# Weight tiles of 256-column products: the first of a block on the activations' remainder of 256 bytes, the later ones 64 bytes off

## The chip, the cores and the metric

The kernel runs on one core of one Trainium2 chip. The metric is the device time of one launch in microseconds. Before the change it is 2145.89 us, the median of three runs from 2144.37 to 2147.65. The profile is of one further execution of the same program, which took 2144.94 us.

## What is computed

The reference is a trunk of two layers in fp32 on 512 tokens of width 2048: first a multi-scale retention with 8 heads, then a latent attention (MLA) with 16 heads. Each layer is normalised, modulated by a conditioning vector, multiplied by a SiLU gate and added to its input. What bears on the change are the two input projections:

```python
def retention_branch(h, pos, w_in, gn_g, w_out):
    proj = h @ w_in                                   # 2048 -> q, k, v, g
    q, k, v, g = jnp.split(proj, [RET_QK, 2 * RET_QK, 2 * RET_QK + RET_WIDTH], axis=-1)
...
def mla_branch(h, pos, w_in, q_norm_g, w_uq, kv_norm_g, w_ukv, w_out):
    proj = h @ w_in                                   # 2048 -> cq, ckv, k_rope, g
    cq, ckv, k_rope, g = jnp.split(
        proj, [MLA_Q_RANK, MLA_Q_RANK + MLA_KV_RANK, MLA_Q_RANK + MLA_KV_RANK + MLA_ROPE], axis=-1)
...
    return (jax.nn.silu(g) * o) @ w_out
```

## The kernel before

Every fp32 product is made of three products in a shorter format: each operand is split into a high part (a cast on ScalarE, ACT) and a low part (the difference, on VectorE, DVE), and high x high, high x low and low x high are added in PSUM. On TensorE each is a weight load (PEld in the profile) of 128x128 and a matmul (PE) that moves 512 or 256 columns of the activations.

Most projections save one product in eight by a scheme of seven block products. For queries and keys of the retention heads 2 to 5 (names qk2 to qk5) and for the gate columns of MLA groups 2 and 3 (g22 and g23) the scheme halves the tokens too, so its matmuls move 256 columns. `seven_rows_steps` makes these six blocks; for every other projection the matmuls move 512 columns, apart from some ends of sums.

A block of `seven_rows_steps` has eight steps, four of a first half (`second` false, u = 0 to 3) and four of a second half. A step of the first half has two weight tiles, e and o, of 1024 columns each in a high and a low copy; it issues four groups of 12 matmuls, named after their PSUM banks: x and s with tile e, z and y with tile o (x, y, s, z in the last of the four). A step of the second half has three groups: x and s with tile o, y with the half-wide tile e (x, s, y in the last). So a block has 4 x 48 + 4 x 36 = 336 matmuls. A name as qk_02e in the profile is head block, first half, u = 2, tile e; the profile leaves the head's number out, so that qk_02e stands for four tiles, and g_02e for two. The 12 matmuls of a group are two row blocks i, two column blocks b and the three partial products (line 924).

Tiles are prepared a step or so ahead: SP issues the loads, ACT casts the high part, DVE forms differences and the low part. The first product with a tile waits for ACT's part; the third one, which is the first that reads the low part, waits for DVE's. The order of ACT, DVE, TensorE and SP is written out by hand (`queued`, `behind`), with these steps one behind the other.

A high and a low copy lie in one pair tile of 2 x 1024 + 16 floats. `part_tiles` takes from a ring of three pair tiles in the base pool and every fourth time from one of the layer's own pool, and `parts_of` begins both copies `at` floats into their half:

```python
EVEN, ASIDE = 16, 0

def pair_tile(pool, tag, name):
    return pool.tile([P, 2 * 1024 + EVEN], F32R, tag=tag, bufs=1, name=name)

def parts_of(pair, shape, at):
    n = math.prod(shape[1:])
    views = [pair[:, 1024 * i + at : 1024 * i + at + n] for i in range(2)]
```

In the built program all activation tiles of these blocks (hT, h2 and their sums) begin 192 bytes past a multiple of 256, and every pair tile 128 bytes past one. A weight tile at EVEN (16 floats, 64 bytes) therefore has the activations' remainder of 256 bytes, and one at ASIDE lies 64 bytes below it. Column blocks are 512 bytes wide and row blocks 1024 or 2048, so the remainder is the same within a tile. Products of 512 columns have their weights at EVEN. The 256-column products of `seven_rows_steps` all have them at ASIDE.

Other places with 256 columns: `tail_block` (line 1406, end of the retention's output) goes through three weight tiles on the activations' remainder and one ASIDE, three matmuls each; `ga_half` (line 1675, the first MLA gate group) follows it with all weights ASIDE.

Between the groups stands little else for TensorE: the head blocks are followed by the 512-column products of the same head (lines 825 to 827, names vg), g22 follows the latent projection (same lines, names vgc) and g23 follows g22. In g23 16 transposes of the latent queries stand behind step u = 2 of the first half and 16 of the latent keys and values behind step u = 0 of the second (line 1790). In g22 the latent norms (lines 1771 to 1774 and 129) run on ACT and DVE between the weight tiles.

Of the kernel before, what the change touches and what calls it, by code (L numbers as in the profile page):

```python
# [16 lines left out]
P = 128  # L17
T = 512
# [31 lines left out]
def hybrid_trunk_kernel(  # L50
# [53 lines left out]
    def tmp(name, shape=(P, T)):  # L104
        return base.tile(list(shape), F32, tag="tmp", bufs=6, name=name)

    def acc(name):
        return psum.tile([P, T], F32, tag="acc", bufs=4, name=name)
# [41 lines left out]
    def rows(w, u, n, c0, cn):  # L150
        return w[u * n * P : (u + 1) * n * P, c0 : c0 + cn].rearrange("(k p) n -> p k n", p=P)
# [67 lines left out]
    EVEN, ASIDE = 16, 0  # L219
# [581 lines left out]
    def turns(raw_tags, own):  # L801

        n = [0, 0]

        def raw_tile(shape, name):
            n[0] += 1
            pool, tag, bufs = raw_tags[n[0] % len(raw_tags)]
            return pool().tile(shape, F32, tag=tag, bufs=bufs, name=f"{name}_r")

        def part_tiles(shape, name, at):  # L810
            n[1] += 1
            return parts_of(next_pair(name) if n[1] % 4 else own(name), shape, at)

        return raw_tile, part_tiles
# [88 lines left out]

        return [step(second, u) for second in (False, True) for u in range(KD // 2)]

    def seven_rows_steps(name, load_half, acts, sums, raw_tile, part_tiles, finish, rows):


        x_, s_, y_, z_, m1, m4, m5 = ([] for _ in range(7))

        def moving(n, p):
            if isinstance(n, tuple):
                kt, th = n
                return tuple(acts[2 * p + kt][:, a, th * H : (th + 1) * H] for a in range(2))
            s = sums[2 * p + (n - 1) // 2]
            return tuple(s[:, (n - 1) % 2, a, :] for a in range(2))

        def product(bank, n, u, w, first):
            for i in range(2):
                a = moving(n, 2 * u + i)  # L920
                for b in range(2):
                    o = bank[:, b * H : (b + 1) * H]
                    for k, (wp, ap) in enumerate(((0, 0), (0, 1), (1, 0))):
                        PE.matmul(  # L924
                            o, w[wp][:, i, b * P : (b + 1) * P], a[ap], start=first and i + b + k == 0, stop=k == 2,
                            skip_group_check=True,
                        )

        def put_by(ps, n):
            m = tmp(n)  # L930
            ACT.copy(m, ps)
            return m

        def parted_halves(hl, n):
            return [tuple(a[:, :, j * H : (j + 1) * H] for a in hl) for j in range(n)]

        def step(second, u):
            n = f"{name}_{int(second)}{u}"
            w = {}

            def load():
                w["o"] = w["e"] = None
                for key, odd_ in (("o", 1), ("e", 0)) if second else (("e", 0), ("o", 1)):
                    js = (1,) if second and key == "e" else (0, 1)
                    w[key] = raw_tile([P, 2, T] if len(js) == 2 else [P, T], f"{n}{key}")
                    v = w[key] if len(js) == 2 else w[key].rearrange("p (i n) -> p i n", i=2)
                    for c, j in enumerate(js):
                        nc.sync.dma_start(v[:, :, c * H : (c + 1) * H], load_half(u, odd_, j))

            def prepare():  # L950
                e, o = w["e"], w["o"]
                if not second:
                    e0, e1, o0, o1 = (t[:, :, j * H : (j + 1) * H] for t in (e, o) for j in range(2))
                    eh, el = part_tiles([P, 2, T], f"{n}e", ASIDE)
                    DVE.tensor_sub(e1, e1, e0)
                    ACT.copy(eh, e)
                    DVE.tensor_sub(o1, o1, e1)
                    DVE.tensor_sub(o0, o0, o1)
                    DVE.tensor_sub(el, e, eh.bitcast(F32))
                    oh, ol = part_tiles([P, 2, T], f"{n}o", ASIDE)  # L960
                    ACT.copy(oh, o)
                    DVE.tensor_sub(ol, o, oh.bitcast(F32))
                    w["b11"], w["t1"] = parted_halves((eh, el), 2)
                    w["t4"], w["t2"] = parted_halves((oh, ol), 2)
                else:
                    oh, ol = part_tiles([P, 2, T], f"{n}o", ASIDE)
                    ACT.copy(oh, o)
                    ev = e.rearrange("p (i n) -> p i n", i=2)
                    DVE.tensor_sub(ev, o[:, :, H:], ev)
                    DVE.tensor_sub(ol, o, oh.bitcast(F32))  # L970
                    eh, el = part_tiles([P, T], f"{n}e", ASIDE)
                    ACT.copy(eh, e)
                    DVE.tensor_sub(el, e, eh.bitcast(F32))
                    w["b21"], w["b22"] = parted_halves((oh, ol), 2)
                    w["t3"] = tuple(a.rearrange("p (i n) -> p i n", i=2) for a in (eh, el))

            def multiply():
                if not second:
                    if u == 0:
                        for l, t in ((x_, "x"), (s_, "s"), (z_, "z"), (y_, "y")):  # L980
                            l.append(acc(f"{t}_{name}"))
                    forms = [(x_, (0, 0), "b11"), (s_, 1, "t1"), (z_, (1, 1), "t4"), (y_, 2, "t2")]
                    if u == NU7 - 1:
                        forms = [forms[i] for i in (0, 3, 1, 2)]
                else:
                    forms = [(x_, (1, 0), "b21"), (y_, 3, "t3"), (s_, 4, "b22")]
                    if u == NU7 - 1:
                        forms = [forms[i] for i in (0, 2, 1)]
                for l, f, k in forms:
                    product(l[0], f, u, w[k], not second and u == 0)  # L990

            def follow():
                if not second and u == NU7 - 1:
                    m1.append(put_by(x_[0], f"m1_{name}"))
                    DVE.tensor_add(y_[0], y_[0], m1[0])
                    m5.append(put_by(s_[0], f"m5_{name}"))
                    DVE.tensor_add(s_[0], y_[0], m5[0])
                if second and u == 0:
                    m4.append(put_by(z_[0], f"m4_{name}"))
                if second and u == NU7 - 1:  # L1000
                    finish(x_[0], s_[0], y_[0], m4[0], m5[0])

            return Step(load, prepare, multiply, follow, rows=rows(second, u))

        NU7 = KD // 4
        return [step(second, u) for second in (False, True) for u in range(NU7)]

    def heads_steps(h):
# [22 lines left out]
    sums2 = {}  # L1031
# [46 lines left out]
    for h in range(1, RH):  # L1078
        if h == 1:
# [4 lines left out]
                sums=lambda u: {0: 2, 1: 3, 2: 4, 4: 5, 5: 6, 6: 7}.get(u),  # L1084
# [428 lines left out]
    h2 = [None] * KD  # L1513
# [128 lines left out]
    def l2_pair(name):  # L1642
        return l2_ready.pop() if l2_ready else pair_tile(pools["l2"], "own", name)
# [161 lines left out]
    turns2 = turns(((lambda: pools["l2"], "bw", 2), (lambda: base, "raw", 3)), lambda name: l2_pair(name))  # L1805
# [5 lines left out]
    def g2_seven(gi):  # L1811


        def load_half(u, odd_, j):
            c0 = 1088 + gi * T + j * H
            return w_mla_in[:, c0 : c0 + H].rearrange("(u i e p) n -> u e p i n", i=2, e=2, p=P)[u, odd_]

        def finish(x, s, y, m4, m5):
            def store(j, half, t):
                r0 = (gi * 4 + 2 * j) * P  # L1820
                POOL.dma_start(
                    sg2_d[r0 : r0 + 2 * P, half * H : (half + 1) * H].rearrange("(b p) n -> p b n", p=P),
                    t.rearrange("p (b n) -> p b n", b=2),
                )

            for j, ps in enumerate((x, s)):
                st = tmp(f"sgs_{gi}_{j}")
                ACT.activation(st, ps, AF.Silu)
                store(j, 0, st)
            for j, m in enumerate((m4, m5)):  # L1830
                DVE.tensor_add(m, m, y)
                ACT.activation(m, m, AF.Silu)
                store(j, 1, m)

        return seven_rows_steps(f"g2{gi}", load_half, h2, sums2, *turns2, finish, lambda second, u: 0)

    g23 = g2_seven(2) + g2_seven(3)

    for n, g_c, at in (("q", qn_s, (0, 4, 10, 11)), ("kv", kvn_c, (1, 5, 12, 13))):
# [655 lines left out]
```

## Time and profile before

| | |
|---|---|
| median of three runs | 2145.89 us |
| lowest and highest | 2144.37, 2147.65 us |
| profiled execution, its own time | 2144.94 us |
| span from first to last instruction | 2143.2 us |
| granted TensorE clock over the span | 0.999 |
| TensorE matmuls and weight loads | 11100 each |
| HBM read and written | 417.96 MB, 43.00 MB |
| matmuls of line 924 | 2016 |

Times in the profile are counted from the span's start. A row of the timeline has the start, the time from the first start to the last end, engine, line, operation, output and inputs, shape and count, and in brackets the engine's idle time before it and what ended it. Matmuls overlap, one's duration is several times the distance to the next, so the speed of a run is read from the starts of two rows and the count between them. In the view by stretch a row has, for each engine, the busy time and the instructions, then the granted clock, the share of the DMA engines and the GB/s that they moved.

### The profile page before, as it was taken

The page shows a single profiled execution, that of the slowest core. Times are in us where ns is not written, and L with a number is a line of the kernel's source. Part 1 is how long each engine was busy: PE and PEld are TensorE (multiplying, and loading weights), DVE is VectorE, ACT ScalarE, POOL GpSimd, SP SyncE. Part 2 cuts the span into 40 slices and gives each one's busy share as a digit, 9 for nine tenths or more (in the row PEclk, how much of TensorE's full clock was granted, in tenths as well). Part 3 has the DMA queues.
Part 4 walks back from the last instruction along what each step waited for, and adds up shares of the span by engine and source line. Part 5 has one row for each costly group of instructions (what it writes and reads, how often), then busy time and mean ns, then how long its engine had stood idle before and what let it go on. Part 6 is the DMA issues. An engine that isn't in the chain of part 4 may idle for free.

```text
span 2143.2 us, 29960 instructions
## 1 busy us (share of the span) xinstructions
PE 2115.7 (99%) x11100; PEld 1816.8 (85%) x11100; DVE 1677.3 (78%) x2481; ACT 1054.5 (49%) x1604; POOL 106.6 (5%) x178
## 2 busy tenths in 40 slices
PE   7999999999999999999999999999999999999998
PEld 5887898988889888888888888898889989988887
DVE  7899788888988789666777777668978788886755
ACT  5764444444444544434344534445446565664434
POOL 1000000000000000000000000010001000000000
PEclk9999999999999999999999999999999999999999
DMA  9975787877788778855647566553466644346734
GB/s 381 397 281 196 223 287 228 273 242 262 252 261 261 236 239 278 262 180 189 236 155 251 178 206 243 167 177 113 163 191 203 188 128 148 119 133 220 246 103 144
DMA packets 229781, 462.95 MB, mean 216 GB/s; under 512 B 20817, under 2 KB 84337, under 8 KB 225793
## 3 DMA queue, kind: packets, MB, share of 16 engines
q1 hardware_dynamic: 217424, 421.85, 60.0%
q0 software_dynamic: 11920, 38.91, 4.7%
q8 instruction: 87, 1.43, 0.3%
q14 instruction: 60, 0.49, 0.1%
q10 hardware_dynamic: 290, 0.27, 0.0%
HBM read 417.96 MB, written 43.00 MB: 215 GB/s over the span
## 4 chain that ended last, share of the span: by engine, by line
PE 85%; DVE 5%; DMA 5%; issue 2%; ACT 1%; POOL 1%; SPq 0%; POOLq 0%; DVEq 0%; ACTq 0%
PE o L1406 11%; PE o L2331 4%; PE s L825 2%; PE x L825 2%; PE x L826 2%; PE y L825 2%; PE s L826 2%; PE y L826 2%; PE s L827 2%; PE x L827 2%; PE y L827 2%; PE s_qk L924 2%; PE x_qk L924 2%; PE y_qk L924 2%; PE qk L160 2%; PE qk L158 2%
## 5 line engine op out<-in xcount | busy, mean ns | idle before, releaser
L1406 PE MATMUL o<-o_h,o_p 128*128 128x512 f32 (+1 forms) x1088 | 323.4, 378 | 0.2 <-DVE o_p L136 0.2
L1406 PEld LDWEIGHTS o<-o_h,o_p 128*128 128x128 f32 x1088 | 199.8, 188 | 38.4 <-DVE o_p L136 1.6
L1406 PE MATMUL o<-o_l,o_p 128*128 128x512 f32 (+1 forms) x544 | 204.8, 377 | 0.0
L1406 PEld LDWEIGHTS o<-o_l,o_p 128*128 128x128 f32 x544 | 102.3, 188 | 18.5
L136 DVE TENSOR_TENSOR o_p<-o_r,o_p 128x1024 fp32r<-128x1024 f32 x64 | 78.1, 1223 | 49.2 <-ACT o_p L135 48.5
L2331 PE MATMUL o<-o_h,o_w 128*128 128x512 f32 (+1 forms) x320 | 82.2, 346 | 0.0
L135 ACT CAST o_p<-o_r 128x1024 fp32r<-128x1024 f32 x64 | 66.5, 1051 | 25.7 <-PE o L1406 18.5
L160 PE MATMUL qk<-hT,qk_p 128*128 128x512 f32 x192 | 74.8, 390 | 1.5 <-DVE qk_p L136 1.5
L378 DVE SCALAR_TENSOR_TENSOR aw<-aw,c_all 128x2048 f32<-128x2048 f32 (+1 forms) x35 | 73.2, 2104 | 2.6 <-DMA aw<-in_ada_t_dram 2.6
L158 PE MATMUL qk<-hT,qk_p 128*128 128x512 f32 x192 | 75.0, 391 | 0.0
L159 PE MATMUL qk<-hT,qk_p 128*128 128x512 f32 x192 | 74.7, 389 | 0.0
L1108 DVE SCALAR_TENSOR_TENSOR mod<-mod,c_odd 128x1024 f32<-128x1024 f32 x48 | 58.1, 1220 | 19.6 <-DMA mod<-in_ada_t_dram 19.6
L2331 PEld LDWEIGHTS o<-o_h,o_w 128*128 128x128 f32 x320 | 55.9, 188 | 7.5
L1108 DVE SCALAR_TENSOR_TENSOR mod<-mod,c_bm 128x1024 f32<-128x1024 f32 x48 | 58.5, 1219 | 0.0
L135 ACT CAST o_h<-o_in 128x1024 fp32r<-128x1024 f32 x24 | 25.3, 1052 | 64.1 <-PE o L159 46.6
L136 DVE TENSOR_TENSOR o_l<-o_in,o_h 128x1024 fp32r<-128x1024 f32 x24 | 29.3, 1222 | 33.5 <-ACT o_h L135 33.5
L2331 PE MATMUL o<-o_l,o_w 128*128 128x512 f32 (+1 forms) x160 | 55.2, 345 | 0.0
L136 DVE TENSOR_TENSOR o_w<-o_w_raw,o_w 128x1024 fp32r<-128x1024 f32 x32 | 38.9, 1220 | 19.2 <-ACT o_w L135 19.2
L1261 ACT ACTIVATE yn<-y,nmr,gn_r 128x512 f32<-128x512 f32 x32 | 22.3, 777 | 62.6 <-DVE nmr L1255 62.6
L159 PE MATMUL o<-o_l,o_w 128*128 128x512 f32 x128 | 49.9, 390 | 0.6 <-DVE o_l L136 0.6
L158 PE MATMUL o<-o_h,o_w 128*128 128x512 f32 x128 | 50.1, 391 | 0.0
L160 PE MATMUL o<-o_h,o_w 128*128 128x512 f32 x128 | 49.8, 389 | 0.0
(1534 smaller groups left out, 6339.2 us busy)
## 6 DMA issues: line engine op xcount, KB each, us to landing
mod<-in_ada_t_dram SPq DMA_DIRECT2D x96, 512.0 KB, 5.9
o_r<-in_ret_w_out_dram SPq DMA_DIRECT2D x64, 512.0 KB, 5.3
aw<-in_ada_t_dram SPq DMA_DIRECT2D x30, 1024.0 KB, 9.3
mod_gate<-in_ada_t_dram SPq DMA_DIRECT2D x32, 512.0 KB, 4.8
o_w_raw<-in_mla_w_out_dram SPq DMA_DIRECT2D x32, 512.0 KB, 4.5
qk_r<-in_ret_w_in_dram SPq DMA_DIRECT2D x48, 256.0 KB, 3.3
qk_r<-qk_d SPq DMA_DIRECT2D x32, 256.0 KB, 6.0
v_r<-v_d SPq DMA_DIRECT2D x32, 256.0 KB, 6.5
```

The costliest lines, as they stand in the source:

```text
L135: ACT.copy(hi, src)
L136: DVE.tensor_sub(lo, src, hi.bitcast(F32))
L158: PE.matmul(o, lhs[0], rhs[0], start=first and not seeded, stop=False, skip_group_check=seeded)
L159: PE.matmul(o, lhs[0], rhs[1], start=False, stop=False, skip_group_check=seeded)
L160: return PE.matmul(o, lhs[1], rhs[0], start=False, stop=last, skip_group_check=seeded)
L825: PE.matmul(banks[b], a[0], w[0], start=first, stop=False, skip_group_check=True)
L826: PE.matmul(banks[b], a[0], w[1], start=False, stop=False, skip_group_check=True)
L827: PE.matmul(banks[b], a[1], w[0], start=False, stop=True, skip_group_check=True)
L924: PE.matmul(o, w[wp][:, i, b * P : (b + 1) * P], a[ap], start=first and i + b + k == 0, stop=k == 2, skip_group_check=True,)
L1108: DVE.scalar_tensor_tensor(out=aw, in0=aw, scalar=1.0, in1=silu_c[j], op0=ALU.mult, op1=ALU.mult, accum_out=mc[:, j, b : b + 1],)
L1406: PE.matmul(o, w[i][:, ki, c0 + b * P : c0 + (b + 1) * P], a[j], start=first and i + j == 0, stop=last and i == 1, skip_group_check=True,)
L2331: PE.matmul(banks2[b][:, cols], w[0][i][:, 0, b * P : (b + 1) * P], o2_moving(w, u, cols)[j], start=u + i + j == 0, stop=u == KD - 1 and i ...
```

## The change

`seven_rows_steps` gets an argument `level`, a set of steps. In a step that is in it, the first of the two tiles (e in the first half, o in the second) is put at EVEN; every other tile stays at ASIDE. The default is the first step of the block, which holds for qk2 to qk5. g22 has the same step; g23 has the last step of its first half and the second step of its second half, the steps behind the two sets of transposes.

```diff
-    def seven_rows_steps(name, load_half, acts, sums, raw_tile, part_tiles, finish, rows):
+    def seven_rows_steps(name, load_half, acts, sums, raw_tile, part_tiles, finish, rows, level=((False, 0),)):
...
         def step(second, u):
             n = f"{name}_{int(second)}{u}"
             w = {}
+            ats = (EVEN if (second, u) in level else ASIDE, ASIDE)
...
                 if not second:
                     e0, e1, o0, o1 = (t[:, :, j * H : (j + 1) * H] for t in (e, o) for j in range(2))
-                    eh, el = part_tiles([P, 2, T], f"{n}e", ASIDE)
+                    eh, el = part_tiles([P, 2, T], f"{n}e", ats[0])
...
-                    oh, ol = part_tiles([P, 2, T], f"{n}o", ASIDE)
+                    oh, ol = part_tiles([P, 2, T], f"{n}o", ats[1])
...
                 else:
-                    oh, ol = part_tiles([P, 2, T], f"{n}o", ASIDE)
+                    oh, ol = part_tiles([P, 2, T], f"{n}o", ats[0])
...
-                    eh, el = part_tiles([P, T], f"{n}e", ASIDE)
+                    eh, el = part_tiles([P, T], f"{n}e", ats[1])
...
-        return seven_rows_steps(f"g2{gi}", load_half, h2, sums2, *turns2, finish, lambda second, u: 0)
+        return seven_rows_steps(
+            f"g2{gi}", load_half, h2, sums2, *turns2, finish, lambda second, u: 0,
+            ((False, 0),) if gi == 2 else ((False, 3), (True, 1)),
+        )
```

## The prediction

> **What bounds the kernel now.** I read the page first (busy shares, granted clock, chain of waits), then the busy time by stretch, then TensorE's timeline around every place where 256-column products stand.
>
> ```profile
> span 2143.2 us, 29960 instructions
> PE 2115.7 (99%) x11100; PEld 1816.8 (85%) x11100; DVE 1677.3 (78%) x2481; ACT 1054.5 (49%) x1604; POOL 106.6 (5%) x178
> ...
> PEclk9999999999999999999999999999999999999999
> ...
> PE 85%; DVE 5%; DMA 5%; issue 2%; ACT 1%; POOL 1%; SPq 0%; POOLq 0%; DVEq 0%; ACTq 0%
> ```
>
> TensorE is busy for 99% of the span at an unthrottled clock and holds 85% of the chain that ended last. A time saved on TensorE counts, unless something else is late in its place.
>
> ```profile
> 282.80:322.40 39.60, 39.60 (x337) 39.56 (x337) 34.18 (x45) 18.94 (x24) 3.82 (x8) 1.00 0.86 288
> ...
> 630.30:669.90 39.60, 39.60 (x337) 39.56 (x337) 34.18 (x45) 18.94 (x24) 4.72 (x9) 1.00 0.87 291
> 1614.50:1697.20 82.70, 82.70 (x706) 82.67 (x705) 66.32 (x89) 49.13 (x75) 5.95 (x7) 1.00 0.60 179
> ```
>
> These are the first and the last of the four head blocks (qk2 to qk5) and the two gate blocks (g22 and g23), with the columns PE, PEld, DVE, ACT, POOL, clock, DMA share and GB/s. PE has no idle time in any of them. A busy PE is not a PE at its peak, though, so the next view gives the distance between starts (the pitch).
>
> ```profile
> 282.84 1.58 PE L924 MATMUL x_qk<-hT,qk_00e 128*128 128x256 f32 x12
> ...
> 288.49 1.58 PE L924 MATMUL x_qk<-hT,qk_01e 128*128 128x256 f32 x12
> ...
> 294.15 1.58 PE L924 MATMUL x_qk<-hT,qk_02e 128*128 128x256 f32 x12
> ...
> 322.41 0.40 PE L825 MATMUL x<-vg_00e,hT 128*128 128x512 f32 x1
> ```
>
> 28 groups of 12 matmuls take 322.41 - 282.84 = 39.57 us, so the pitch is 39.57/336 = 117.8 ns, and it is even: 5.65 us for each 48. All weights in this block lie ASIDE, 64 bytes below the activations' remainder of 256 bytes. The same shape with the same 64 bytes runs faster elsewhere in this trace:
>
> ```profile
> 1441.30 0.28 PE L1406 MATMUL o<-o_l,o_p 128*128 128x256 f32 x1
> 1441.41 0.28 PE L1406 MATMUL o<-o_h,o_p 128*128 128x256 f32 x1
> 1441.53 4.02 PE L1675 MATMUL g<-h,g_p 128*128 128x256 f32 x34
> 1445.38 0.50 PE L1139 MATMUL x_sums<-ones,x_ss 128*128 128x1 f32 x4
> ```
> ```profile
> 1449.24 11.22 PE L1675 MATMUL g<-h,g_p 128*128 128x256 f32 x96 [0.35 <-ACT h L1528]
> ```
> ```profile
> 1450.21 10.25 PE L1675 MATMUL g<-h,g_p 128*128 128x256 f32 x89
> 1460.30 0.40 PE L158 MATMUL g<-h,g_p 128*128 128x512 f32 x1
> ```
>
> 34 matmuls of the first MLA gate block take 3.85 us, 113.2 ns each; later 89 take 10.09 us, 113.4 ns. So one arrangement of operands has two lasting rhythms, 117.8 and 113.3 ns, and which one holds depends on how the run began. What stands ahead of the run at 1441.53 is the point: the last products of the retention's output, in which nine matmuls with weights on the activations' remainder alternate with three whose weights lie ASIDE.
>
> ```profile
> 1417.52 0.40 PE L1406 MATMUL o<-o_h,o_p 128*128 128x256 f32 x2
> ...
> 1418.24 0.40 PE L1406 MATMUL o<-o_h,o_p 128*128 128x256 f32 x2
> 1418.48 0.28 PE L1406 MATMUL o<-o_l,o_p 128*128 128x256 f32 x1
> 1418.59 0.40 PE L1406 MATMUL o<-o_h,o_p 128*128 128x256 f32 x2
> ```
> ```profile
> L1406 PEld LDWEIGHTS o<-o_h,o_p 128*128 128x128 f32 x129 | 20.0, 191 | 0.1
> L1675 PEld LDWEIGHTS g<-h,g_p 128*128 128x128 f32 x144 | 16.7, 188 | 0.5 <-ACT h L1528 0.5
> ```
>
> From 1417.52 to 1418.24 six matmuls on the same remainder take 0.72 us, 120 ns each, and their weight loads are longer (191 against 188 ns on average). From 1418.48 to 1418.59, on the ASIDE tile right behind them, it is 0.11 us. In the old order the qk block comes straight from 512-column products into ASIDE tiles and lands in 117.8. With the change it passes through 24 matmuls on the same remainder first, as the output products do.
>
> **The change, part by part.** It removes and adds no instruction, wait or DMA, and no engine's order moves; it moves the two halves of seven weight tiles by 64 bytes (four head blocks, g22 once, g23 twice). ACT's casts and DVE's subtractions write to the shifted places with the same shapes; I cost them at nothing, and if that were wrong DVE's 34.18 of 39.60 us leaves 5.4 us of cover in a head block.
>
> Head blocks. The first tile (00e) feeds 24 matmuls at 120: 2.88 us. The other 312 run at 113.3: 35.35 us. Sum 38.23 us instead of 39.57, a gain of 1.34 us, four times 5.36 us. Bounds: the pitch behind the tile is between 113.3 (seen behind such tiles) and 120 (never leaving the tile's own), so a block lies between -1.34 and +0.75 us; I take the first end, since the rows at 1418.48 and 1441.53 are the same sequence.
>
> Whether DVE and DMA follow: 34.18 us of DVE in 38.23 is 89%, and the DMA share goes from 0.86 to 0.89. The tightest tiles are 01e and 02e:
>
> ```profile
> 286.81 1.22 DVE L959 TENSOR_TENSOR qk_01e<-qk_01e_r,qk_01e 128x1024 fp32r<-128x1024 f32 x1
> ...
> 292.42 1.22 DVE L959 TENSOR_TENSOR qk_02e<-qk_02e_r,qk_02e 128x1024 fp32r<-128x1024 f32 x1
> ```
> ```profile
> 1909.20 0.68 DVE L2036 TENSOR_TENSOR o<-o,sg 128x512 f32<-128x512 f32 x1
> ...
> 1909.93 0.19 PEld L158 LDWEIGHTS a<-ukT,uqT 128*128 128x128 f32 x1 [0.89 <-DVE o L2036]
> ```
>
> DVE's low part is read by the third matmul, whose load begins one pitch after the first starts. For 02e that is 294.15 + 0.12 = 294.27, and DVE ends at 293.64. The hand-over from DVE to a waiting load is 0.05 us in the last two rows (1909.88 to 1909.93). TensorE will be 0.27 us earlier at 02e (72 matmuls x 4.5 ns, less 24 x 2.2 ns for the first tile), which leaves 0.31 us. At 01e, with 0.58 us before the hand-over and a gain of 0.06, 0.47 are left.
>
> Behind the blocks the wide products take over, and the gain must live there:
>
> ```profile
> 670.00:905.00 235.00, 235.00 (x1038) 194.30 (x1037) 199.84 (x256) 110.98 (x133) 14.67 (x27) 1.00 0.77 250
> ```
>
> PE is busy for all of 235 us after the last head block with DVE at 85% and DMA at 0.77: nothing there takes the gain back.
>
> Gate block g22. Here DVE and ACT do the latent norms between the weights, in a chain that starts at the end of the block before and no longer hangs on TensorE:
>
> ```profile
> 1614.05 0.69 DVE L1764 TENSOR_TENSOR q<-m_c,yc 128x512 f32<-128x512 f32 x1 [0.83 <-PE yc L827]
> ...
> 1622.22 0.17 DVE L129 TENSOR_SCALAR q_r_v<-ss_q 128x4 f32<-128x4 f32 x1 [1.16 <-ACT q_sq L1774]
> ...
> 1628.08 0.17 DVE L129 TENSOR_SCALAR kv_r_v<-ss_kv 128x4 f32<-128x4 f32 x1 [1.24 <-ACT kv_sq L1774]
> ...
> 1630.22 1.22 DVE L959 TENSOR_TENSOR g_03e<-g_03e_r,g_03e 128x1024 fp32r<-128x1024 f32 x1
> ```
> ```profile
> 1614.53 1.58 PE L924 MATMUL x_g<-h,g_00e 128*128 128x256 f32 x12
> ...
> 1631.49 1.58 PE L924 MATMUL x_g<-h,g_03e 128*128 128x256 f32 x12
> ```
>
> The low part of 03e is done at 1631.44, and its reader's load begins at 1631.61 now: 0.17 us to spare. With the change TensorE gains 16.96 - (2.88 + 120 x 0.1133) = 0.48 us up to there and asks at 1631.13. It waits until 1631.49, hand-over included, 0.36 us, and keeps 0.12 of the 0.48. This is the step where the gain is not free: queued behind that load are all later matmuls of g22. What rhythm holds after the wait is the unknown. Two bounds, from rows of this trace:
>
> ```profile
> 1671.06 1.91 PE L1790 MATMUL qT<-ident,q 128*128 128x128 f32 x16
> 1672.73 1.66 PE L924 MATMUL x_g<-h,g_03e 128*128 128x256 f32 x12
> ...
> 1682.71 1.91 PE L1790 MATMUL kvT<-ident,kv 128*128 128x128 f32 x16
> 1684.37 1.66 PE L924 MATMUL x_g<-h,g_11o 128*128 128x256 f32 x12
> ...
> 1697.17 0.40 PE L158 MATMUL uq<-qT,uq_p 128*128 128x512 f32 x1
> ```
>
> After the transposes, 84 ASIDE matmuls take 9.98 us (118.8 with the restart): an interrupted run comes back slow. The run that began behind a wait at 1449.24 was at 113.4 from 1450.21 on. From 03e to the first transposes stand 333 matmuls, so the wait leaves between 0 and 333 x 4.5 ns = 1.50 us. [...]
>
> Gate block g23 starts anew twice. Behind the first transposes 24 of 84 matmuls are on the remainder and 60 can be fast: 60 x 4.5 - 24 x 2.2 ns = 0.22 us. Behind the second, 24 of 108: 0.33 us. Together 0.55 us, with bounds of -0.10 (no switch, 48 x 2.2 ns lost) and 0.55.
>
> Sum: 5.36 + 0.12 + 0.55 = 6.03 us. The profiled execution took 2144.94 us, which becomes 2138.9; that execution lies 0.95 us under the median of the runs shown (2145.89), by which the answer is **2139.9 us**.
>
> **Rivals.** (1) The same, but the 113 rhythm survives the wait in g22: 1.50 us more, 2138.4. For it: the row at 1450.21. Against: both restarts after transposes.
>
> (2) The place of a weight tile changes nothing and 117.8 stays: 2145.9. For it: nothing else in the head blocks differs between tiles, and the four blocks agree with each other, so the rhythm could be the block's own. Against: 120, 117.8 and 113.3 ns for one shape. [...]
>
> (3) Slower: the rhythm of 120 outlives the tile. Place: all 2016 matmuls of line 924, from the first tile on; price 2016 x 2.2 ns = 4.4 us, 2150.3. It decides from the first ASIDE matmul of qk2. Against it: the pitch of 0.11 at 1418.48, right behind such a tile. For it: that spell was 9 matmuls long and this one is 24.
>
> (4) The switch comes, but a short wait in the head blocks (02e has 0.31 us) undoes it about halfway: half of 5.36 is kept and g23's 0.55, so 3.2 us, 2142.7. For it: DMA at 0.86 and DVE at 86% in those blocks; against: ACT and DVE work for later tiles hangs on TensorE's own ends and moves forward with it.
>
> **How the numbers follow.** The forecast has 0.50, rival 1 0.25, rival 2 0.08, rival 3 0.05, rival 4 0.12. The likeliest gives 2139.9. The range runs from 2136.8 (rival 1, on the lowest run before, 2144.37, instead of the median) to 2143.2, a little above rival 4; outside are rivals 2 and 3 with 0.13 and some spread of the runs. The forecast's own range is 2138.4 to 2141.4, from the runs' spread of 1.5 us. 0.2%, about what a measurement of this kernel can tell from no change, is 4.3 us: faster means below 2141.6. Forecast and rival 1 lie there (0.75), and a third of rival 4's spread: faster 0.80. Within 0.2%: rival 2 and the rest of rival 4, 0.15. Slower: rival 3, 0.05.
>
> **What would show it.** In the new profile the first 24 matmuls of each head block start 120 ns apart and the block is 38.2 us long, with pitch 113.3 from the third group of 12 on. TensorE idles or stretches one pitch by 0.36 us at tile 03e of g22, and the groups after it show whether 1.41 us (forecast) or 1.36 us (rival 1) is the length of 12. In g23 the second and the fourth group behind the first transposes are short. PE stays without idle time from 282 to 905 us. Wrong would be: 1.41 us groups throughout (rival 2), 1.44 us groups (rival 3), or a switch back within a head block (rival 4).

## The result, and the profile after

| | before | after |
|---|---|---|
| median (lowest to highest), 15 runs each | 2145.91 us (2144.05 to 2147.65) | 2141.67 us (2139.38 to 2143.99) |
| ratio of the times, 95% interval | | 0.9979, 0.9972 to 0.9987 |
| profiled execution, its own time and span | 2144.94, 2143.2 us | 2141.7, 2139.9 us |

The kernel is 4.24 us faster, by the interval 2.8 to 6.0 us. From the page of the changed kernel, the lines that answer to those shown of before (span, busy shares, chain of waits):

```profile
span 2139.9 us, 29960 instructions
PE 2114.4 (99%) x11100; PEld 1814.4 (85%) x11100; DVE 1676.8 (78%) x2481; ACT 1054.2 (49%) x1604; POOL 106.4 (5%) x178
...
PE 20%; DMA 1%; DVE 1%; issue 1%; ACT 0%; POOL 0%; POOLq 0%; DVEq 0%
```

TensorE is the bound as before. The chain adds up to some 23% only: it could be followed back from the end for that part and says nothing of the stages with 256 columns. These have to be read from the timeline. TensorE around the first head block (qk2), start and time from first start to last end of each group:

```profile
284.49 1.60 PE L924 MATMUL x_qk<-hT,qk_00e 128*128 128x256 f32 x12
...
287.37 1.52 PE L924 MATMUL z_qk<-hT,qk_00o 128*128 128x256 f32 x12
288.73 1.52 PE L924 MATMUL y_qk<-sums,qk_00o 128*128 128x256 f32 x12
...
322.73 0.40 PE L825 MATMUL x<-vg_00e,hT 128*128 128x512 f32 x1
...
324.57 0.39 PE L827 MATMUL s<-vg_00e,sums 128*128 128x512 f32 x1
325.11 0.47 PE L825 MATMUL s<-vg_00e,sums 128*128 128x512 f32 x1 [0.15 <-DVE m_qk L1071]
```

The first tile's 24 matmuls take 287.37 - 284.49 = 2.88 us (120 ns), every group behind it 1.36 us (113.3 ns), and the block 322.73 - 284.49 = 38.24 us where it took 39.57. Ten products further on there is something new: 0.54 us between two starts that are 0.23 us apart elsewhere. TensorE waits some 0.31 us for DVE's sum m_qk, and it does so behind each of the four head blocks (0.54, 0.53, 0.54 and 0.54 us between the two starts). The view of waits from 275 to 905 us, empty for the kernel before, has one line now (us in total, times, longest; two of the four are short of being counted as idle, because a product's 0.39 us lies over most of the 0.53 or 0.54 us):

```profile
PE s L825 <- DVE m_qk L1071: 0.3, 2, 0.2
```

TensorE's timeline of after in the gate blocks, g22 (first five rows) and g23 (from its first transposes on):

```profile
1612.37 1.60 PE L924 MATMUL x_g<-h,g_00e 128*128 128x256 f32 x12
...
1627.48 1.52 PE L924 MATMUL y_g<-sums,g_02o 128*128 128x256 f32 x12
1628.84 1.94 PE L924 MATMUL x_g<-h,g_03e 128*128 128x256 f32 x12
1630.62 1.58 PE L924 MATMUL y_g<-sums,g_03o 128*128 128x256 f32 x12
1632.03 1.58 PE L924 MATMUL s_g<-sums,g_03e 128*128 128x256 f32 x12
...
1668.78 1.91 PE L1791 MATMUL qT<-ident,q 128*128 128x128 f32 x16
1670.44 1.68 PE L924 MATMUL x_g<-h,g_03e 128*128 128x256 f32 x12
1671.96 1.52 PE L924 MATMUL y_g<-sums,g_03o 128*128 128x256 f32 x12
1673.33 1.60 PE L924 MATMUL s_g<-sums,g_03e 128*128 128x256 f32 x12
...
1694.36 0.40 PE L158 MATMUL uq<-qT,uq_p 128*128 128x512 f32 x1
```

And one row of its weight loads in the same trace, with the idle time ahead of it:

```profile
1629.33 1.24 PEld L924 LDWEIGHTS x_g<-h,g_03e 128*128 128x128 f32 x10 [0.30 <-DVE g_03e L960]
```

In g22 the groups are 1.36 us long up to 03e, whose low part comes late; behind that wait they are 1.41 us again. In g23, behind the transposes, the groups without the tile on the remainder are short (1.37 us from 1671.96 to 1673.33).

Where the time went is best seen in two stretches, measured between the starts of the same matmuls in both traces. "Heads" runs from the first product of qk2 to one product behind the 512-column products of the fourth head (qk<-hT,qk_p of line 159; 904.91 before, 902.76 after): 622.07 us before, 618.27 after. "Gates" runs from the first product of g22 to the first product behind g23: 82.64 before (1614.53 to 1697.17), 81.99 after (1612.37 to 1694.36). The heads gain 3.80 us and the gates 0.65, together 4.45, close to the 4.24 of the medians. The spans differ by only 3.3 us mainly because of one disturbance ahead of any changed tile, in this row by stretch of after (engines' busy time, then granted clock, DMA share, GB/s):

```profile
164.00:170.00 6.00, 6.00 (x21) 4.74 (x20) 5.62 (x11) 2.38 (x5) 2.14 (x4) 0.72 0.88 291
```

The granted clock of this trace is 0.50 from 164.45 to 167.80 and 0.72 from 167.80 to 167.90, which makes 3.4 us at 0.50 and the 0.72 of the row. The 512-column products start 0.43 us apart there and 0.23 behind it, and TensorE is 1.6 us later from there on; it is no part of the change.

### The profile page after: what moved, and what is told of

It reads as the page before. It is cut to its first block, busy times and chain, and to the rows that moved or that the text cites. A ratio compares the mean times of both kernels' runs of the same rounds, so it can differ in the third digit from the quotient of the medians.

```text
span 2139.9 us, 29960 instructions
## 1 busy us (share of the span) xinstructions
PE 2114.4 (99%) x11100; PEld 1814.4 (85%) x11100; DVE 1676.8 (78%) x2481; ACT 1054.2 (49%) x1604; POOL 106.4 (5%) x178
## 3 DMA queue, kind: packets, MB, share of 16 engines
q8 instruction: 87, 1.43, 0.3%
```

## The experiments

Each was built from the kernel before or after by the edit shown. The last two columns are the two stretches of the trace, as the difference to the kernel before. Times of single variants lie 1 us or so apart, within each other's intervals; what tells them apart are the stretches and the pitches, and the times say that the sums are right.

| run | median, us (runs) | before, us | ratio, 95% interval | heads | gates |
|---|---|---|---|---|---|
| the change | 2141.67 (15) | 2145.91 | 0.9979, 0.9972 to 0.9987 | -3.80 | -0.65 |
| heads_only | 2141.61 (10) | 2146.08 | 0.9979, 0.9970 to 0.9988 | -3.93 | +0.01 |
| all_even | 2150.21 (10) | 2146.08 | 1.0018, 1.0008 to 1.0027 | +2.77 | +1.47 |
| off32 | 2140.28 (1) | 2146.08 | | -4.14 | -0.15 |
| all_off32 | 2143.04 (1) | 2145.06 | | -1.08 | -0.33 |
| middle | 2142.49 (1) | 2146.29 | | -2.23 | -0.64 |
| g22_again | 2141.24 (8) | 2146.29 | 0.9974, 0.9963 to 0.9984 | -3.88 | -2.00 |
| both | 2139.32 (5) | 2146.08 | 0.9968, 0.9955 to 0.9980 | -4.33 | -1.99 |
| follow_first | 2140.39 (9) | 2146.29 | 0.9974, 0.9965 to 0.9984 | -4.19 | -0.67 |
| before_follow | 2146.43 (10) | 2146.29 | 1.0002, 0.9993 to 1.0011 | +0.97 | +0.01 |
| moved | 2139.20 (5) | 2145.95 | 0.9968, 0.9956 to 0.9981 | -5.50 | -0.61 |
| before_moved | 2144.66 (10) | 2145.95 | 0.9995, 0.9985 to 1.0004 | -0.44 | 0.00 |
| best | 2138.13 (5) | 2145.95 | 0.9966, 0.9953 to 0.9978 | -5.72 | -2.00 |

### What sets the pitch

**heads_only** takes the change back in the gate blocks:

```diff
-            ((False, 0),) if gi == 2 else ((False, 3), (True, 1)),
+            (),
```

> The shifted first tile stays in the four head blocks; g22 and g23 have all weights ASIDE again. My theory (the rhythm is set by a run of weights on the activations' remainder followed by weights off it, block by block): head blocks of 38.2 us with 113.3 ns behind tile 00e, g22 and g23 at 117.8 ns throughout and no wait at 03e of g22. Time: 4 x (1.34 less the 0.31 us that TensorE now waits at the second s bank of the wide block behind) = 4.1 us under before, about 2141.8. Rival (the rhythm, once set, is kept by TensorE across the wide products): g22 would begin at 113.3 without a shifted tile, and the time would be nearer to 2141.0.

The head blocks were as in the changed kernel. In g22 every group has 1.41 us, and nothing is late at 03e, as TensorE's timeline of heads_only shows:

```profile
1627.30 1.58 PE L924 MATMUL x_g<-h,g_03e 128*128 128x256 f32 x12
1628.71 1.58 PE L924 MATMUL y_g<-sums,g_03o 128*128 128x256 f32 x12
```

So the fast rhythm was not carried from the head blocks across the 512-column products into the gates: behind them g22 has 1.41 us a group without a tile of its own and 1.36 with one. The wait for m_qk stayed, which belongs to the head blocks.

**all_even** puts all tiles of the six blocks on the activations' remainder:

```diff
-            ats = (EVEN if (second, u) in level else ASIDE, ASIDE)
+            ats = (EVEN, EVEN)
```

> All weight tiles of the six blocks on the activations' remainder. My theory: 120 ns throughout, 40.3 us for a head block, 2016 x 2.2 ns = 4.4 us over before, 2150.3. Rival (the remainder costs only when it alternates with another place): 113.3 or 117.8 throughout, 2138 to 2146.

All groups are 1.44 us long, the rows of TensorE's timeline of all_even:

```profile
284.54 1.60 PE L924 MATMUL s_qk<-sums,qk_00e 128*128 128x256 f32 x12
285.98 1.60 PE L924 MATMUL z_qk<-hT,qk_00o 128*128 128x256 f32 x12
```

The price of rival 3 was right: 2.77 + 1.47 = 4.24 us slower by the stretches, 4.13 by the medians. In these blocks a tile on the remainder costs 120 ns a matmul as long as it is used; it pays only through what it leaves behind, 113.3 ns in the changed kernel.

**off32** puts the first tile 32 bytes off the remainder, halfway to ASIDE:

```diff
-            ats = (EVEN if (second, u) in level else ASIDE, ASIDE)
+            ats = (8 if (second, u) in level else ASIDE, ASIDE)
```

> The first tile of each block is shifted by 32 bytes instead of 64, so it lies neither on the activations' remainder nor where the later tiles lie. My theory (the tile must share the remainder, whose longer weight loads push the loads out of step with the matmuls): no switch, the first 24 matmuls at 117.8 or 113.3 but not 120, and the blocks at 117.8, 39.6 us; time as before, 2145.9. Rival (any change of a weight tile's place between neighbours resets the rhythm): 113.3 behind tile 00e, blocks of 38.1 to 38.2 us, time as the changed kernel, 2141.7.

TensorE's timeline of off32, the beginning of qk2 and a place in g22:

```profile
282.51 1.56 PE L924 MATMUL x_qk<-hT,qk_00e 128*128 128x256 f32 x12
...
285.31 1.52 PE L924 MATMUL z_qk<-hT,qk_00o 128*128 128x256 f32 x12
...
1621.11 1.59 PE L924 MATMUL x_g<-h,g_02e 128*128 128x256 f32 x12
1622.54 1.58 PE L924 MATMUL s_g<-sums,g_02e 128*128 128x256 f32 x12
```

DVE's timeline of off32, the low part of the same tile 02e:

```profile
1619.98 1.22 DVE L960 TENSOR_TENSOR g_02e<-g_02e_r,g_02e 128x1024 fp32r<-128x1024 f32 x1
```

My theory that only the same remainder switches fell here: behind the first tile the head blocks go at 113.3 ns (1.36 us a group) as with the change. But the switch does not hold everywhere. In g22 the groups are 1.36 us up to 02e. Its low part is done at 1621.20, and with the 0.05 us of hand-over 0.02 us too late for the load that reads it (due at 1621.11 + 0.12 = 1621.23): the distance from the third start to the fourth is 134 ns in place of 113, the group takes 1.43 us, and 1.41 us groups follow. In g23, behind the transposes, no group of this kernel is short. Within the tile the starts are 118, 118, 116, 117, 120, 114, 115, 118, 120, 113, 116, 118, 120, 113, ... ns apart: a cycle of about four matmuls.

**all_off32** asks whether that cycle ever settles (`ats = (8, 8)` in the same line):

> Every weight tile of the six blocks lies 32 bytes off the activations' remainder instead of 64 (none is on it). Seen so far: a single such tile in front of a block gave pitches that wander between 113 and 120 ns, about 116.5 on average over 24 matmuls. My theory (32 bytes off no rhythm is stable; the phase between loads and matmuls drifts round and round): the pitch wanders through the whole block, 116 to 117 ns on average, a head block of 39.0 to 39.3 us, and a time of 2143 to 2145 beside a kernel before of 2145.9. Rival A (the phase stays in the first good place it meets): 113.3 ns from some early matmul on, head blocks near 38.2 us, time near 2140. Rival B (all that counts is to be off the remainder): 117.8 ns as in the kernel before, 2145.9.

The same places in TensorE's timeline of all_off32:

```profile
284.32 1.56 PE L924 MATMUL s_qk<-sums,qk_00e 128*128 128x256 f32 x12
285.73 1.56 PE L924 MATMUL z_qk<-hT,qk_00o 128*128 128x256 f32 x12
...
1630.99 1.57 PE L924 MATMUL y_g<-sums,g_03o 128*128 128x256 f32 x12
1632.40 1.57 PE L924 MATMUL s_g<-sums,g_03e 128*128 128x256 f32 x12
```

It doesn't: 118, 120, 113, 116 and so on through whole blocks, 116.7 ns on average (1.40 us a group), so my theory held and both rivals fell. Behind one short wait at 03e of g22 even this became another cycle, 116, 118, 119, 116, 118, 120, 115, 119 ns, 117.8 on average (1.41 us a group), until the transposes in g23.

**middle** has the tile on the remainder third instead of first in the head blocks (`level=((False, 2),)` as the default):

> The changed kernel, but in the four head blocks the tile on the activations' remainder is the third of the first half's e tiles (02e) instead of the first (00e); g22 gets it there too by the default only where its own argument doesn't say otherwise, so g22 and g23 stay as changed. My theory (the tile sets the rhythm of what follows it, wherever it stands): the first 96 matmuls of a head block go at 117.8, 24 at 120 (or a little under), the other 216 at 113.3: a block takes 11.31 + 2.88 + 24.47 = 38.66 us, 0.43 more than with the tile in front, and the four blocks gain 3.6 us in place of 5.3. Rival (the rhythm is settled by how a block begins, behind the 512-column products, and not by the tile): 117.8 behind the tile too, 39.6 us a block, or 113.3 from the first matmul, 38.1 us.

TensorE's timeline of middle around the tile:

```profile
292.44 1.57 PE L924 MATMUL y_qk<-sums,qk_01o 128*128 128x256 f32 x12
293.85 1.59 PE L924 MATMUL x_qk<-hT,qk_02e 128*128 128x256 f32 x12
295.27 1.60 PE L924 MATMUL s_qk<-sums,qk_02e 128*128 128x256 f32 x12
296.72 1.52 PE L924 MATMUL z_qk<-hT,qk_02o 128*128 128x256 f32 x12
```

1.41 us a group ahead of the tile, 1.42 and 1.45 with it, 1.36 behind it: the tile sets the rhythm, not the beginning of the block. The heads gained 2.23 us and not the 3.6 of the blocks, since this kernel waits for m_qk too.

**g22_again** adds the late tile of g22, 03e, to those on the remainder:

```diff
-            ((False, 0),) if gi == 2 else ((False, 3), (True, 1)),
+            ((False, 0), (False, 3)) if gi == 2 else ((False, 3), (True, 1)),
```

> The changed kernel with one edit: in g22 the tile 03e, whose reader waits 0.36 us, is on the activations' remainder too, as 00e is. My theory (the rhythm behind a wait is whatever the restart falls into, and a tile on the remainder always leads into 113.3): 03e takes 24 matmuls at 120 ns behind the wait, and the other matmuls up to g22's end and into g23 up to the first transposes go at 113.3 instead of 117.8, 24 x 2.2 ns lost and about 300 x 4.5 ns gained, 1.3 us; time 1.3 us under the changed kernel, 2140.4 beside a kernel before of 2145.9. Rival (after a wait the run stays at 117.8 whatever stands there): 0.05 us more than the changed kernel, 2141.8.

TensorE's timeline of g22_again, the groups behind the wait:

```profile
1630.98 1.52 PE L924 MATMUL y_g<-sums,g_03o 128*128 128x256 f32 x12
1632.34 1.60 PE L924 MATMUL s_g<-sums,g_03e 128*128 128x256 f32 x12
1633.78 1.52 PE L924 MATMUL z_g<-h,g_03o 128*128 128x256 f32 x12
```

Behind the same wait the groups are 1.36 us now, but for the tile's own second group (1.44). The gates gain 2.00 us in place of 0.65, 1.35 more, as the theory had it (1.3). The median's gain over the changed kernel, 2141.24 against 2141.67, is smaller than that and within the runs' spread.

### What TensorE waits for behind a head block

Three rows of the kernel before, from the timelines of ACT, DVE and TensorE around the end of qk2:

```profile
318.48 1.05 ACT L859 CAST vg_00o<-vg_00o_r 128x1024 fp32r<-128x1024 f32 x1 [3.30 <-PE s_qk L924]
...
322.99 1.28 DVE L1070 TENSOR_TENSOR m_qk<-m_qk,y_qk 128x512 f32<-128x512 f32 x2
...
324.46 0.42 PE L825 MATMUL s<-vg_00e,sums 128*128 128x512 f32 x1
324.72 0.39 PE L826 MATMUL s<-vg_00e,sums 128*128 128x512 f32 x1
```

And the rows of ACT and DVE at the same place in the changed kernel (TensorE's stand above):

```profile
319.17 1.05 ACT L859 CAST vg_00o<-vg_00o_r 128x1024 fp32r<-128x1024 f32 x1 [3.35 <-DVE vg_00o_r L856]
...
322.54 1.22 DVE L1109 SCALAR_TENSOR_TENSOR mod<-mod,c_bm 128x1024 f32<-128x1024 f32 x1
...
323.68 1.28 DVE L1071 TENSOR_TENSOR m_qk<-m_qk,y_qk 128x512 f32<-128x512 f32 x2
```

The two sums m_qk read the PSUM banks y of the block that ends, and the tenth wide product, the first into its bank, waits for them. Before, they ended at 324.27 and the product started at 324.46: 0.19 us apart, and the next start is 0.26 instead of 0.23 us later. After, the product would be due at 324.57 + 0.23 = 324.80, but the sums end at 324.96 and it starts at 325.11, 0.15 us behind them. With that hand-over the slack before was 0.04 us. DVE did not follow TensorE's whole gain: against the start of the wide products the sums end 2.23 us later now and ended 1.86 us later before. A modulation piece of 1.22 us stands ahead of them, and ACT's cast of vg_00o, on which DVE's next work hangs, was released by TensorE before and is released by DVE itself now.

**both** and **follow_first** put the sums ahead of the modulation piece (`both` with the edit of g22_again as well):

```diff
-            return Step(load, prepare, multiply, follow, rows=rows(second, u))
+            res = Step(load, prepare, multiply, follow, rows=rows(second, u))
+            res.ends = second and u == NU7 - 1
+            return res
...
+        if getattr(step, "ends", False):
+            with behind(V_, A_, T_):
+                step.follow()
+            step.follow = lambda: None
```

> The changed kernel with two edits: at the end of a head block the sums that free the PSUM bank (m_qk) are queued on DVE ahead of the modulation piece instead of behind it, and g22 has a second shifted tile, 03e, where TensorE waits. My theory: the waits of 0.31 us at the second s bank go (4 x 0.31 = 1.24 us), and in g22 the 288 matmuls behind 03e run at 113.3 instead of 117.8 (1.3 us less 0.05 for the tile): 2.5 us under the changed kernel, 2139.2. Rival (the gain is taken back by the next wait: DVE is late for the tiles of the wide block, or for g23): 2140.5 to 2141.7.

> The changed kernel with one edit: at the end of each head block the two sums m_qk (which set the PSUM bank of the second wide group behind the block free) stand on DVE ahead of the modulation piece of 1.22 us instead of behind it. Operands of TensorE stay as in the changed kernel. My theory (the 0.31 us that TensorE waits for this bank, four times, are a term of their own that the head blocks' gain turned into): the wait at s<-vg_00e is gone in all four blocks and the time lies 0.4 to 1.2 us under the changed kernel, 2140.5 to 2141.3 beside a kernel before of 2145.9; the lower gain if the modulation piece, now later, delays the parts of the next wide tiles (vg_01e, vg_02e) as it did in the kernel with both edits. Rival (the wait is only where TensorE meets a limit that lies further back, DVE's amount of work in the stretch): the wait moves as a whole to vg_01e or vg_02e, and the time stays at 2141.7.

The wait at s<-vg_00e went in both. It came back further on in both, at vg_01e and vg_02e behind each of the four blocks. So both, at 2139.32 us, met the 2139.2 expected by luck: its stretches gain 6.32 us where 4.45 + 2.5 = 6.95 were expected, and its runs lie 2.3 us apart. For follow_first, two rows of DVE's timeline:

```profile
320.96 1.28 DVE L1073 TENSOR_TENSOR m_qk<-m_qk,y_qk 128x512 f32<-128x512 f32 x2 [0.30 <-PE y_qk L924]
...
330.95 1.22 DVE L857 TENSOR_TENSOR vg_02e<-vg_02e_r,vg_02e 128x1024 fp32r<-128x1024 f32 x1
```

And two of TensorE's weight loads:

```profile
331.52 0.41 PEld L825 LDWEIGHTS x<-vg_02e,hT 128*128 128x128 f32 x2
332.23 0.19 PEld L826 LDWEIGHTS x<-vg_02e,hT 128*128 128x128 f32 x1 [0.30 <-DVE vg_02e L857]
```

DVE now stands idle for 0.30 us until the block's last products are done, works without a break from there, and ends the low part of vg_02e at 332.17; the load that reads it starts at 332.23. Of the 1.25 us of waits taken away, 0.39 is left as gain in the heads (-4.19 against -3.80). Neither side of the expectation was right as it stood: the wait moved, but not as a whole. (The planned order of TensorE moved as well: two products with the high part stand in a row there, the "x2" above.)

**before_follow** does the same to the kernel before (all tiles ASIDE):

> The kernel before (every tile 64 bytes off) with the two sums m_qk ahead of the modulation piece at the end of each head block. My theory: the bank is free just in time there already, so the order buys nothing without the faster head blocks: 2145.9, within 0.4 us of the kernel before. Rival (the order on DVE is better in itself): 0.4 to 1.2 us faster, 2144.7 to 2145.5, with TensorE's starts behind the head blocks earlier than in the kernel before.

The order is no gain in itself; by the trace it costs 0.97 us in the heads, for the reason just shown, while the time is the same within its interval.

**moved** leaves the order and takes work away: the two modulation pieces of each head that fall on the end of the block and the step behind it are loaded and added later (at 345.27 and 356.15 us behind the first block, behind the parts of vg_05 and vg_07).

```diff
-            lambda second, u: int(second and (u % 2 == 1 or (h > 5 and u in (2, 4)))),
+            lambda second, u: int(u % 2 == 1 or (h > 5 and u in (2, 4))) if second else int(1 < h < 6 and u in (3, 5)),
...
-            f"qk{h}", load_half, hT, sums1, *turns1, finish, lambda second, u: int(second),
+            f"qk{h}", load_half, hT, sums1, *turns1, finish, lambda second, u: int(second and u < 2),
```

> The changed kernel, but the two modulation pieces of 1.22 us that DVE does at the end of each head block and one step later (322.54 and 329.32 in the changed kernel's trace) stand four and six steps further on, among the 512-column products, where DVE was busy for 81% of the stretch and not 97%. Operands of TensorE and the order of the sums m_qk against the end of the block stay. So far: with the sums put ahead of the piece the wait of 0.31 us at s<-vg_00e went, but 0.17 and 0.35 us came back at vg_01e and vg_02e, whose low parts DVE delivers late. My theory now (what the head blocks' gain meets is the amount of DVE work in the 20 us behind a block, and any order of it only moves the wait): with 2.4 us less of it there, neither s<-vg_00e nor vg_01e nor vg_02e waits, TensorE's gain up to 900 us is the full 5.3 us (3.8 in the changed kernel), and the time lies 1.0 to 1.5 us under the changed kernel, 2140.2 to 2140.7 beside a kernel before of 2145.9. Rival (the PSUM bank's release is late in itself, by the sums' place behind the end of the block): 0.31 us stays at s<-vg_00e, four times, and the time is that of the changed kernel, 2141.7.

One row of DVE's timeline of moved, and two of TensorE's:

```profile
321.22 1.28 DVE L1071 TENSOR_TENSOR m_qk<-m_qk,y_qk 128x512 f32<-128x512 f32 x2 [0.31 <-PE y_qk L924]
...
323.08 0.39 PE L825 MATMUL s<-vg_00e,sums 128*128 128x512 f32 x1
323.31 0.39 PE L826 MATMUL s<-vg_00e,sums 128*128 128x512 f32 x1
```

The sums end at 322.50, 0.58 us ahead of the product that needs the bank, and the next start is 0.23 us behind it. The heads gain 5.50 us, the 5.3 of the blocks and a little of the uneven pitches that were there before. In follow_first a new order alone only moved the wait; here, with less work and no other order, it is gone. DVE's amount of work behind the block was the limit, as the theory said.

**before_moved** (all tiles ASIDE, pieces moved) and **best** (moved and g22_again together):

> The kernel before (every tile of the six blocks 64 bytes off) with the two modulation pieces moved as in the kernel above. My theory: nothing waits for DVE behind the head blocks of the kernel before, so moving the pieces buys nothing: 2145.9, within 0.4 us. Rival (the moved pieces are a gain of their own): 1.0 us faster, 2144.9, with TensorE's starts earlier behind each head block.

> The kernel with the moved modulation pieces and the second tile on the remainder in g22 (03e). My theory: both gains add, 1.2 us behind the head blocks and 1.3 us in g22, 2139.0 to 2139.4 beside a kernel before of 2145.9 (ratio 0.9968). Rival (a later limit takes part of it back, at 1909 us or 2035 us, where all kernels so far have waits that vary by 0.3 to 0.8 us): 2140 to 2141.

The move alone gives 0.44 us in the heads, the uneven pitches at the same product, right behind it and at vg_02e. So the kernel before did lose a little there, which the expectation had at nothing. The time, 2144.66 us, is nearer the rival's 2144.9 than the 2145.9 expected, but it isn't told apart from no change. With the fast blocks it is worth 1.70 (-5.50 against -3.80). best has the lowest median, 2138.13 us; its stretches give 7.72 us, its median 7.82.

## Why the prediction was right, and which term was off

The forecast was 6.03 us less, 2139.9 us; 4.24 were measured, 2141.67 us. That lies inside the whole range, but 0.3 us above the forecast's own part of it (2138.4 to 2141.4). Its direction and the mechanism in the blocks held, and one term was missing.

- **Head blocks.** 38.23 us forecast, 38.24 measured, 24 matmuls at 120 ns and the rest at 113.3. Rivals 2 and 3 fell with it; all_even, all_off32 and the kernel before show that the place counts: 120, 116.7 and 117.8 ns for one program whose tiles lie 0, 32 and 64 bytes off. That it is the distance to the activations which counts was not shown: no run moved the activations, and the weights' own remainder of 256 bytes (192, 160 and 128) fits the three pitches as well.
- **DVE and DMA follow.** Inside the head blocks nothing waited, as forecast. Rival 4 put a wait there; its 2142.7 us is near the measured time, but the lost part went elsewhere.
- **Behind the blocks.** This is the step that failed: "PE is busy for all of 235 us after the last head block with DVE at 85% and DMA at 0.77: nothing there takes the gain back." Four times 0.31 us, 1.25 in all, were taken back at s<-vg_00e. The sign "PE stays without idle time from 282 to 905 us" failed with it. The blocks gained 1.34 us each, 5.35, and the heads 3.80; the remaining 0.30 went in slightly longer pitches, most of it right behind the waits. The busy share of these 235 us did not show the slack of one product in the first 2 us behind a block (0.04 us behind qk2); I had asked that question (when is the operand ready, when is it read) at 01e, 02e and 03e, but not of the PSUM banks at the blocks' ends. The stretched start at 324.46 of the kernel before showed the answer. The experiments moved the wait and, with 2.4 us of DVE work gone from there, removed it.
- **g22.** Gain up to 03e 0.48 forecast, 16.96 - 16.47 = 0.49 measured; wait 0.36, measured 1.78 - 1.41 = 0.37 against the same group before; kept 0.12, measured 0.12. The open question, what rhythm holds behind the wait, came out slow (117.8), against rival 1: the sum has nothing for the matmuls behind it, the lower end of the bounds, and that is what was measured. Ahead of the result no run showed this term, and why the wait was followed by this rhythm none shows now: in off32 some 0.02 us of delay at 02e went with the same switch, and behind the wait at 1449.24 in the kernel before the starts were 226, 118, 117, 119 and 160 ns apart and then 113.4, so that slow restart did not last. So this term was partly luck. g22_again shows what the slow rhythm cost: 1.35 us.
- **g23.** 0.55 forecast; from the first transposes to the end 25.58 us in place of 26.11, 0.53.

With the missing terms the sum would have been 6.03 - 1.25 - 0.30 = 4.48 us.

## What to carry to other kernels

When a stage gets faster, ask of its successor, for the first few products, when each operand and each PSUM bank comes free and how long before use: here TensorE had no idle time before, and the slack of 0.04 us showed only in one distance of 0.26 us in place of 0.23. If reordering moves a wait, as follow_first did from vg_00e to vg_01e and vg_02e, look at the amount of work of the engine behind it: here the wait went when two pieces of 1.22 us left the place. Read a pitch over groups of equal instructions: here one kind of matmul had even rhythms of 113.3 and 117.8 ns with its weights at the same place, and a tile of 24 matmuls at 120 ns set the faster one for those behind it.

## What the runs showed of the hardware that I had not expected

- The pitch of a run of 256-column matmuls depended on the place of the weights and on what went before. The places tried are 0, 32 and 64 bytes below the activations' remainder of 256 bytes; whether the distance counts or the weights' own remainder, no run tells. On the remainder it was 120 ns. 64 bytes off it was one of two: 113.3 ns behind both groups of a tile on the remainder, in every block seen, and 117.8 behind 512-column products, transposes or the late load in g22 (though behind the wait at 1449.24 in the kernel before for three distances only: one of 160 ns followed, and 113.4 behind it). One group on the remainder does not always do: in moved, behind the first transposes of g23, the group between the tile's two still took 1.42 us, and the 1.36 came behind the second, as TensorE's timeline of moved shows:

```profile
1668.73 1.57 PE L924 MATMUL y_g<-sums,g_03o 128*128 128x256 f32 x12
1670.15 1.60 PE L924 MATMUL s_g<-sums,g_03e 128*128 128x256 f32 x12
1671.58 1.52 PE L924 MATMUL z_g<-h,g_03o 128*128 128x256 f32 x12
```

- 32 bytes off it was a cycle of about 118, 120, 113, 116 ns, and where that leaves the next tiles differed: 113.3 in the head blocks and at the start of g22, 117.8 in g23. Why the place counts, no run shows.
- The wait of 0.37 us in g22, worth three matmuls, was followed by 4.5 ns more on each of some 300 matmuls: a second tile on the remainder won 1.35 us back. In off32 some 0.02 us of delay was followed by the same pitch.
- The granted clock of after fell to 0.50 for 3.4 us at about 164 us (0.72 in the row of 6 us), behind an idle time of TensorE that is the same 1.54 us in the trace of before, where the row has 1.00. In g22_again the row has 0.78, behind the same 1.54 us; in follow_first, middle, all_off32 and moved it has 1.00, behind 1.54 us as well. The row of after:

```profile
163.50 0.50 PE L160 MATMUL qk<-hT,qk_p 128*128 128x512 f32 x1 [1.54 <-DVE qk_p L136]
```

  What decides it between runs with the same idle time was not tried.
